# The operands of TensorE's products lie 144 bytes further in SBUF

## The chip, the cores and the metric

The kernel runs on one core of one Trainium2 chip. The time is the device time of one launch in microseconds, from three runs; one more execution is profiled. A core has TensorE (PE in the profile; PEld is its weight load), VectorE (DVE), ScalarE (ACT), GpSimd (POOL) and the queues that issue transfers (SP's above all). SBUF is the on-chip memory of 128 partitions; an address below is a byte offset in each partition.

## The reference, cut to what matters

One inference step over 256 prompt tokens and 32 sample tokens (288 columns in the kernel), through one layer: a feed-forward block, a mixer of two gated recurrences, and a second feed-forward block, each between normalisations, in float32.

```
def swiglu(x, w_in, w_out):
    gate, up = jnp.split(x @ w_in, 2, axis=-1)
    return (jax.nn.silu(gate) * up) @ w_out
...
    x = x + 0.5 * rmsnorm(swiglu(rmsnorm(x, g[0]), ffn1_w_in[l], ffn1_w_out[l]), g[1])
    m, sg, sh = hybrid_mixer(rmsnorm(x, g[2]), mix_w_in[l], ...)
    x = x + rmsnorm(m, g[3])
    x = x + 0.5 * rmsnorm(swiglu(rmsnorm(x, g[4]), ffn2_w_in[l], ffn2_w_out[l]), g[5])
```

The model width is 2048 and the feed-forward width 5632. The change touches none of the arithmetic; it matters only that nearly all work is the matrix products of these three parts.

## The kernel before

**Products in three parts.** A float32 operand is split into a high half (rounded to the type fp32r) and a low half (the rest), and a product is the sum of high by high, high by low and low by high. So every weight tile of 128 x 128 takes part in three matmuls of 128 x 288.

**Units and blocks.** Weights come from HBM in units of 128 x 1024 values (512 KB): two row groups of 128, an even and an odd one, by 512 columns. `Weights.load` (L93) issues the transfer into one of three buffers `raw`; `Weights.pieces` (L120) splits it into one of four buffers `wh`, ScalarE writing the high half (L137) and VectorE the low half (L138). `block` (L626) takes 8 units where the operand is `xhl` (the split input, 16 row groups; the groups gate, up, qk, v, hfq, hi and mo of the profile) and accumulates four PSUM tiles of 128 x 288. For each unit `two` (L640) issues six matmuls per PSUM tile, so 24 per unit, all at L647. The output product of the feed-forward blocks (group out) reads the split hidden tile `hid` instead and takes 2 units per block, over four blocks `o` of output columns; 192 of its matmuls in a row stand for one chunk of 512 hidden columns. An even chunk uses the first two places below, an odd chunk the last two; a few blocks take all four.

**Where the operands lie.** Call 16 bytes (4 values) a line, and count lines within 256 bytes, so 0 to 15. `tiles` (L51) lays out `xhl`, `hid` and the tile for the early products (`fill`) in the same way: the row groups of four successive units start 0, 27, 9 and 18 lines from each other's common start (`PART`, L37), and the reading order of a matmul (`turns_of`, L48) goes through eight places that lie 36 lines apart before it moves on by one line. `Weights.add` (L89) gives the four units of a pass the offsets 7, 2, 0 and 9 lines in their weight buffer (`AHEAD_LINES`, L38). Together with small unused tiles ("gap") at the head of some pools this makes the odd row group's high half begin at the same line in the weights and in the input. For the four units that follow each other these lines are 5, 0, 14 and 7, and then 5 again. The other halves of a unit lie at fixed distances from them, the same for every unit. The weight buffers are 8448 bytes apart, 33 times 256, so that a unit's line does not depend on its buffer.

**What sets the order.** The program is written out by Python once; each engine's instructions stand in that order, and semaphores between engines are placed by the framework from the tiles that are written and read. There is no cost model.

Of the kernel before, what the change touches and what calls it, by code (L numbers as in the profile page):

```python
# [9 lines left out]
F32 = mybir.dt.float32  # L10
F32R = mybir.dt.float32r
# [5 lines left out]
P = 128  # L17
TP = 256
TS = 32
T = TP + TS  # L20
# [13 lines left out]
LINE = 4  # L34
PLACES = 8
# [15 lines left out]
def tiles(pool, n, name):  # L51

    q = n // 2 * T
    t = pool.tile([P, LINE + 10 * LINE + 4 * q], F32R, name=name, tag=name, bufs=1)
    hs, ls = [None] * n, [None] * n
    for dst, odd, at in ((hs, 1, 0), (hs, 0, q + 4 * LINE), (ls, 1, 2 * q + 10 * LINE), (ls, 0, 3 * q + 10 * LINE)):
        r = t[:, LINE + at:LINE + at + q].rearrange("p (b g j c) -> p b g j c", g=PLACES, j=4, c=T // PLACES)
        for u in range(n // 2):
            dst[2 * u + odd] = r[:, u // 4, :, PART[u % 4], :]
    return hs, ls  # L60
# [6 lines left out]
def apart(t, step):  # L67

    return bass.AP(t.tensor, t.offset, [list(t.ap[0]), [step, 2], list(t.ap[1])])


class Weights:
# [47 lines left out]
    def pieces(self, n):  # L120

        i = self.split
        raw = self.raws.pop(i)
        pool = self.extra if i in self.extra_units else self.hlp
        hl = pool.tile([P, 2112], F32R, name=f"wh{i}", tag="wh")
        at = self.at[i]
        low = hl[:, at + ODD_LOW:at + ODD_LOW + 2 * (EVEN_LOW - ODD_LOW)]
        l = low.rearrange("p (a c) -> p a c", a=2)[:, ::-1, 0:512]
        h = apart(hl[:, at:at + 512], ODD_HIGH)
        self.parts[i] = (h, l)  # L130
        self.split += 1
        raw = raw.rearrange("p (a b) -> p a b", b=512)
        for j in range(n):
            a = slice(0, 2) if n == 1 else slice(2 * j // n, 2 * j // n + 1)
            w = min(512, 1024 // n)
            c = slice(j * w % 512, j * w % 512 + w)
            i1 = self.nc.scalar.activation(h[:, a, c], raw[:, a, c], AF.Copy).ins  # L137
            i2 = self.nc.vector.tensor_tensor(l[:, a, c], raw[:, a, c], h[:, a, c].bitcast(F32), op=ALU.subtract).ins  # L138
            self.recent = i1, i2
            yield i1, i2  # L140
# [27 lines left out]
def trunk_kernel(ctx, tc, x_prompt, x_sample, state_gla, state_hgrn, norm_gains, f1_in, f1_out, f2_in, f2_out,  # L168
# [6 lines left out]
    xpool = ctx.enter_context(tc.tile_pool(name="xpool", bufs=1))  # L175
# [69 lines left out]
    def wider(n):  # L245

        return {i for i in range(n - 44, n + 4) if i // 2 % 3 == (n + 2) // 2 % 3}
# [38 lines left out]
    x = [xpool.tile([P, T], F32, name=f"x{k}") for k in range(KT)]  # L286
    yg = [xpool.tile([P, 4, T], F32, name=f"y{k}") for k in range(4)]
    y = [yg[k // 4][:, k % 4, :] for k in range(KT)]
    xh, xl = tiles(xpool, KT, "xhl")
    rt = xpool.tile([P, T], F32, name="rt")  # L290
    rp = xpool.tile([P, T], F32, name="rp")
# [224 lines left out]
    class PreNorm:  # L516
# [3 lines left out]
        def __init__(self, name, update, ahead, at):  # L520

            self.name, self.update, self.ahead, self.at, self.late = name, update, ahead, at, []
            self.tmps = None
# [25 lines left out]
    class Fill:  # L549
# [3 lines left out]
        def __init__(self, pool, name, gains, gnext, some, ahead):  # L553
            self.gnext, self.name, self.some, self.ahead = gnext, name, some, ahead
            pool.tile([P, 8], F32, name=f"{name}gap")

            both = list(zip(*tiles(pool, 2 * EARLY, f"{name}hl")))
            self.tiles = [both[:EARLY], both[EARLY:]]
            self.gains = pool.tile([P, 32], F32, name=f"{name}g")[:, 0:EARLY]
            V.tensor_tensor(self.gains, gains[:, 0:EARLY], prm[:, gnext * KT:gnext * KT + EARLY], op=ALU.mult)  # L560
# [146 lines left out]
    def ffn(tag, gcol, gnext, pn, before, fill=None):  # L707
# [2 lines left out]
        border = []  # L710
        with ExitStack() as pools:
            fp = pools.enter_context(tc.tile_pool(name=f"ffn{tag}", bufs=2))
            fp.tile([P, 32], F32, name=f"gap_f{tag}", bufs=1)
            hid, final_tiles = {}, []
            hidden = tiles(fp, 8, f"hid{tag}")

            def do_in(c):
# [1007 lines left out]
    class Border:  # L1725


        def __init__(self, n, gains, gnext, some, ahead=0):
            self.pools = ExitStack()
            top = self.pools.enter_context(tc.tile_pool(name=f"top{gnext}", bufs=1, side="right"))  # L1730
            top.tile([P, 88], F32, name=f"gap{gnext}")
            W.begin_extra(self.pools.enter_context(tc.tile_pool(name=f"hx{gnext}", bufs=2, side="right")), wider(n))
            self.fill = Fill(self.pools.enter_context(tc.tile_pool(name=f"fl{gnext}", bufs=1, side="right")),
                             f"fill{gnext}", gains, gnext, some, ahead)

    pn = pre1 = PreNorm("pre1", x_first, FIRST, 11)
    pn.late.append(prm2)
    u, border = ffn(1, lambda k: hg1[:, k:k + 1], 2, pn, first)
    u, border = mixer(PreNorm("pre2", u, UPDATED, 11), border)
    ffn(2, lambda k: hg1[:, KT + k:KT + k + 1], None, PreNorm("pre3", u, UPDATED, 11), border.pools, border.fill)  # L1740


# [39 lines left out]
```

## Time and profile before

| what | value |
|---|---|
| median of 3 runs | 2148.63 us (2147.24 to 2149.55) |
| time of the profiled execution | 2147.9 us |
| its span, first to last instruction | 2146.1 us |
| PE busy | 2134.7 us, 99% of the span |
| DVE, ACT busy | 1379.6 us (64%), 1016.8 us (47%) |
| mean granted clock of TensorE | 0.999 |
| matmuls at L647 | 15456 |

The profile's page gives the busy time of each engine, the span in 40 slices, the DMA queues, the chain of work that ended last (followed back from the last instruction), and the costliest groups of instructions. The ends of matmuls are modelled and overlap the next matmul's start, so PE's busy share does not tell how fast it runs; how long a row of matmuls lasts does.

### The profile page before, as it was taken

Reading aid. Unit: us, or ns where it says so; the run is one execution under the profiler, and the core shown is the slowest. Engines: PE = TensorE matmul, PEld = TensorE weight load, DVE = VectorE, ACT = ScalarE, POOL = GpSimd, SP = SyncE. Lnnn points to the kernel's source line nnn. Section 1 sums busy time; section 2 is a strip of 40 time slices with the busy share of each in tenths; the row PEclk is TensorE's granted clock in tenths of the full one; section 3 lists DMA queues with packets and bytes.
Section 4 is the critical chain, followed back from the end, with each engine's and each line's share of the span. In section 5 each row is a group of like instructions: output and inputs, shape, how many; then the busy total and the mean of one; then the engine's idle time right before and its main releaser. Section 6 shows DMA issues by size and latency. Waiting matters only on the chain.

```text
span 2146.1 us, 43224 instructions
## 1 busy us (share of the span) xinstructions
PE 2134.7 (99%) x17828; PEld 2115.5 (99%) x17828; DVE 1379.6 (64%) x2253; ACT 1016.8 (47%) x1537; POOL 180.5 (8%) x327
## 2 busy tenths in 40 slices
PE   9999999999999999999999999999999999999998
PEld 9999999999999999999999999999999999999998
DVE  7655546655665568888888755854665466556656
ACT  6453433343344445655676654644334333433344
POOL 2000000000000001333110000000000020122005
PEclk9999999999999999999999999999999999999999
DMA  7665555555556654678666664555555565666556
GB/s 222 180 177 176 171 176 176 176 171 177 175 176 188 179 175 139 199 211 221 178 188 183 184 190 145 161 176 176 176 177 172 175 186 177 183 186 186 176 171 163
DMA packets 227334, 384.87 MB, mean 179 GB/s; under 512 B 21362, under 2 KB 60864, under 8 KB 227136
## 3 DMA queue, kind: packets, MB, share of 16 engines
q1 hardware_dynamic: 213872, 365.02, 56.7%
q0 software_dynamic: 10992, 16.77, 3.0%
q8 instruction: 140, 2.29, 0.4%
q10 hardware_dynamic: 2272, 0.31, 0.1%
q14 instruction: 58, 0.48, 0.1%
HBM read 363.75 MB, written 11.80 MB: 175 GB/s over the span
## 4 chain that ended last, share of the span: by engine, by line
PE 93%; DVE 3%; ACT 2%; issue 1%; DMA 1%; POOL 0%; DVEq 0%; ACTq 0%; POOLq 0%
PE gate L647 26%; PE out L647 24%; PE up L647 24%; PE hfq L647 5%; PE mo L647 4%; PE hi L647 2%; PE v L647 2%; ACT wh L137 1%; DVE wh L138 1%; PE gate L637 1%; PE gate L636 0%; PE gate L638 0%; PE os L1401 0%; PE sc L1147 0%; ACT ls L202 0%
## 5 line engine op out<-in xcount | busy, mean ns | idle before, releaser
L138 DVE TENSOR_TENSOR wh<-raw,wh 128x1024 fp32r<-128x1024 f32 (+1 forms) x676 | 821.4, 1216 | 572.2 <-ACT wh L137 571.2
L137 ACT ACTIVATE wh<-raw 128x1024 fp32r<-128x1024 f32 (+1 forms) x676 | 709.9, 1052 | 886.5 <-PE gate L647 275.9
L647 PE MATMUL gate<-xhl,wh 128*128 128x288 f32 x4584 | 588.3, 288 | 1.2 <-DVE u L740 0.8
L647 PEld LDWEIGHTS gate<-xhl,wh 128*128 128x128 f32 x4584 | 582.0, 187 | 2.8 <-issue 0.7
L647 PE MATMUL out<-hid,wh 128*128 128x288 f32 x4224 | 532.5, 286 | 0.0
L647 PEld LDWEIGHTS out<-hid,wh 128*128 128x128 f32 x4224 | 530.2, 187 | 0.1
L647 PE MATMUL up<-xhl,wh 128*128 128x288 f32 x4152 | 527.9, 287 | 0.0
L647 PEld LDWEIGHTS up<-xhl,wh 128*128 128x128 f32 x4152 | 525.3, 187 | 0.0
L831 DVE TENSOR_TENSOR y<-out,y 128x288 f32<-128x288 f32 x287 | 116.8, 451 | 73.2 <-PE out L647 73.1
L647 PE MATMUL hfq<-xhl,wh 128*128 128x288 f32 x768 | 103.3, 290 | 0.0
L647 PEld LDWEIGHTS hfq<-xhl,wh 128*128 128x128 f32 x768 | 98.6, 187 | 0.9
L788 POOL DMA_DIRECT2D xT<-b x64 | 37.2, 587 | 733.2 <-PE gate L647 550.6
L647 PE MATMUL mo<-xhl,wh 128*128 128x288 f32 x768 | 97.6, 288 | 0.2 <-ACT y L1715 0.2
L647 PEld LDWEIGHTS mo<-xhl,wh 128*128 128x128 f32 x768 | 97.1, 187 | 0.5 <-ACT y L1715 0.4
L991 POOL MEMSET ahl<- 128x512 f32 x1 | 0.5, 525 | 782.6 <-PE out L647 782.6
L742 ACT ACTIVATE hid<-u 128x288 fp32r<-128x288 f32 x88 | 37.5, 445 | 59.5 <-DVE u L741 58.0
L740 DVE TENSOR_TENSOR u<-up,rt 128x288 f32<-128x288 f32 x88 | 37.8, 451 | 29.2 <-PE up L647 29.2
L647 PE MATMUL hi<-xhl,wh 128*128 128x288 f32 x384 | 53.5, 291 | 0.0
L735 DVE TENSOR_TENSOR g<-gate,rt 128x288 f32<-128x288 f32 x80 | 33.6, 454 | 30.7 <-PE gate L647 30.7
L647 PEld LDWEIGHTS hi<-xhl,wh 128*128 128x128 f32 x384 | 50.2, 188 | 0.5
L647 PE MATMUL v<-xhl,wh 128*128 128x288 f32 x360 | 49.4, 290 | 0.0
L202 ACT ACTIVATE g<-g 128x288 f32<-128x288 f32 x88 | 36.0, 436 | 25.6 <-DVE g L735 25.2
(409 smaller groups left out, 1525.3 us busy)
## 6 DMA issues: line engine op xcount, KB each, us to landing
raw<-in_ffn_w_in_dram SPq DMA_DIRECT2D x350, 512.0 KB, 3.8
raw<-in_ffn_w_out_dram SPq DMA_DIRECT2D x176, 512.0 KB, 3.7
raw<-in_mix_w_in_dram SPq DMA_DIRECT2D x64, 512.0 KB, 4.4
raw<-in_mix_w_in_dram SPq DMA_DIRECT2D x96, 256.0 KB, 3.4
raw<-in_mix_w_out_dram SPq DMA_DIRECT2D x32, 512.0 KB, 3.8
out_dram<-s POOLq DMA_DIRECT2D x32, 256.0 KB, 3.0
s<-in_state_gla_dram SPq DMA_DIRECT2D x16, 256.0 KB, 6.3
s<-in_state_hgrn_dram SPq DMA_DIRECT2D x16, 256.0 KB, 5.8
```

Source lines behind the costliest of these rows:

```text
L137: i1 = self.nc.scalar.activation(h[:, a, c], raw[:, a, c], AF.Copy).ins
L138: i2 = self.nc.vector.tensor_tensor(l[:, a, c], raw[:, a, c], h[:, a, c].bitcast(F32), op=ALU.subtract).ins
L202: ins = S.activation(out, in_, func, **kw).ins
L637: yield lambda: PE.matmul(dst, w[0][:, a, c], parts[1], start=False, stop=False)
L647: product[0] = PE.matmul(dst, w[low][:, a, c], part, start=k == n == 0, stop=k == nk - 2 and n == 5).ins
L735: V.tensor_tensor(g, ps, rt, op=ALU.mult)
L740: ins = V.tensor_tensor(u, ps, rt, op=ALU.mult).ins
L742: S.activation(hh[f], columns(u), AF.Copy)
L788: queues[n % len(queues)].dma_start(dst[q * TS:(q + 1) * TS, 4 * g:4 * g + 4, :, cols].rearrange("p k t c -> p (k t) c"), b32[rows, q])
L831: V.tensor_tensor(y[k], ps, y[k], op=ALU.add)
L991: G.memset(ahl[:, 512:].bitcast(F32), 0.0)
```

## The change

Five lines. The tiles for `xhl`, `hid` and `fill` lose one unused line at their head, and the unused tiles in front of them grow, or one is added (`gap_x`), so that the data begins 144 bytes, which is 9 lines, further than before. Everything in a weight buffer moves one line further inside the buffer, and the buffers themselves move by 128 bytes because of the added tile, so also by 144 bytes. For the tiles at the right end of the memory (`fill` and the extra weight buffers in the pools `hx`) the larger gap moves the address 112 bytes down, which is the same 9 lines within 256 bytes.

| operand | start before | start after | move |
|---|---|---|---|
| `xhl` | 55632 | 55776 | +144 |
| `hid` | 147280 | 147424 | +144 |
| `fill` | 193360 | 193248 | -112 |
| `wh`, first buffer, with its offset of one line after | 108672 | 108816 | +144 |
| extra `wh` in `hx`, first buffer, likewise | 212096 | 211984 | -112 |
| `raw`, first buffer | 96192 | 96320 | +128 |
| `g`, `u` of the feed-forward blocks, `sq`, mixer tiles | | | +128 |
| `x`, `y`, and the mixer's pool `scan` | | | 0 |

The four successive units now begin at lines 14, 9, 7 and 0. Built, the two programs hold the same 24652 instructions in the same order on every engine, with the same shapes, steps and semaphores; only addresses differ (and the numbers in tile names).

```diff
@@ def tiles(pool, n, name):
-    t = pool.tile([P, LINE + 10 * LINE + 4 * q], F32R, name=name, tag=name, bufs=1)
+    t = pool.tile([P, 10 * LINE + 4 * q], F32R, name=name, tag=name, bufs=1)
...
-        r = t[:, LINE + at:LINE + at + q].rearrange("p (b g j c) -> p b g j c", g=PLACES, j=4, c=T // PLACES)
+        r = t[:, at:at + q].rearrange("p (b g j c) -> p b g j c", g=PLACES, j=4, c=T // PLACES)
@@ Weights.pieces
-        at = self.at[i]
+        at = LINE + self.at[i]
@@ trunk_kernel
+    xpool.tile([P, 40], F32, name="gap_x")
     xh, xl = tiles(xpool, KT, "xhl")
@@ ffn
-            fp.tile([P, 32], F32, name=f"gap_f{tag}", bufs=1)
+            fp.tile([P, 40], F32, name=f"gap_f{tag}", bufs=1)
@@ Border
-            top.tile([P, 88], F32, name=f"gap{gnext}")
+            top.tile([P, 120], F32, name=f"gap{gnext}")
```

## The prediction

> **What bounds the kernel now.** I read the page first, its busy times and the chain that ended last.
>
> ```profile
> span 2146.1 us, 43224 instructions
> PE 2134.7 (99%) x17828; PEld 2115.5 (99%) x17828; DVE 1379.6 (64%) x2253; ACT 1016.8 (47%) x1537; POOL 180.5 (8%) x327
> PE 93%; DVE 3%; ACT 2%; issue 1%; DMA 1%; POOL 0%; DVEq 0%; ACTq 0%; POOLq 0%
> ```
>
> TensorE is the bound nearly throughout, and it hardly waits: the span less its busy time is 11.4 us. So the time can move only if a matmul takes longer or shorter. The groups of instructions tell how many there are: all L647 groups that read `xhl`, and the one that reads `hid`.
>
> ```profile
> L647 PE MATMUL gate<-xhl,wh 128*128 128x288 f32 x4584 | 588.3, 288 | 1.2 <-DVE u L740 0.8 <-ACT xhl L300 0.5
> L647 PE MATMUL out<-hid,wh 128*128 128x288 f32 x4224 | 532.5, 286 | 0.0
> L647 PE MATMUL up<-xhl,wh 128*128 128x288 f32 x4152 | 527.9, 287 | 0.0
> L647 PE MATMUL hfq<-xhl,wh 128*128 128x288 f32 x768 | 103.3, 290 | 0.0
> L647 PE MATMUL mo<-xhl,wh 128*128 128x288 f32 x768 | 97.6, 288 | 0.2 <-ACT y L1715 0.2
> L647 PE MATMUL hi<-xhl,wh 128*128 128x288 f32 x384 | 53.5, 291 | 0.0
> L647 PE MATMUL v<-xhl,wh 128*128 128x288 f32 x360 | 49.4, 290 | 0.0
> L647 PE MATMUL qk<-xhl,wh 128*128 128x288 f32 x216 | 29.1, 290 | 0.0
> ```
>
> Those that read `xhl` add up to 4584 + 4152 + 768 + 768 + 384 + 360 + 216 = 11232. Four units of 24 matmuls are a pass, so that is 117 passes; an up or gate block is two. The chain in order of time shows that blocks with equal work differ in length:
>
> ```profile
> 375.42 24.21 PE up L647 x192
> 399.63 23.98 PE out L647 x192
> 423.61 24.23 PE gate L647 x192
> 447.84 24.21 PE up L647 x192
> 472.05 24.03 PE out L647 x192
> ```
>
> Each row is 192 matmuls of one form. An up block takes 24.21 us, an out group of an even chunk 23.98, one of an odd chunk 24.03. To see why, I cut the up block at 375 us at the first matmul of each unit of its first pass, whose lines are 5, 0, 14 and 7 (columns: the stretch, its length, PE's busy time and the count of matmuls that touch it, the granted clock, DMA).
>
> ```profile
> 375.25:378.25 3.00, 3.00 (x24) 1.00 0.59 175
> 378.25:381.24 2.99, 2.99 (x27) 1.00 0.59 175
> 381.24:384.32 3.08, 3.08 (x26) 1.00 0.58 176
> 384.32:387.36 3.04, 3.04 (x26) 1.00 0.54 172
> ```
>
> The same 24 matmuls take 3.00 us at line 5, 2.99 at 0, 3.08 at 14 and 3.04 at 7, 12.11 together, and the second pass brings the block to the 24.21 of the chain. The clock is 1.00 in all four and the DMA share alike, so it is not the clock. The counts run over 24 because a matmul's modelled end reaches into the next unit; the cuts are at starts. The out groups show the same lines in other company: the even chunk goes 5, 0, 5, 0 and the odd one 14, 7, 14, 7.
>
> ```profile
> 399.47:402.46 2.99, 2.99 (x24) 1.00 0.56 181
> 402.46:405.45 2.99, 2.99 (x26) 1.00 0.12 28
> 405.45:408.47 3.02, 3.02 (x27) 1.00 0.79 246
> 471.89:474.88 2.99, 2.99 (x24) 1.00 0.56 182
> 474.88:477.90 3.02, 3.02 (x27) 1.00 0.12 30
> ```
>
> Here the unit at 14 follows one at 7 and takes 2.99, not 3.08. So the slow unit is no property of line 14 alone, but of 14 **after** 0: I read it as a state that TensorE's reads carry from one unit into the next.
>
> **The change part by part.** No instruction is added, removed or moved, so no count times duration changes by itself.
>
> Moving `raw` by 128 bytes and the results of gate and up by 128, with `x` and `y` left in place, alters what ScalarE and VectorE read beside what they write. Their share of a unit is covered:
>
> ```profile
> L138 DVE TENSOR_TENSOR wh<-raw,wh 128x1024 fp32r<-128x1024 f32 (+1 forms) x676 | 821.4, 1216 | 572.2 <-ACT wh L137 571.2
> L137 ACT ACTIVATE wh<-raw 128x1024 fp32r<-128x1024 f32 (+1 forms) x676 | 709.9, 1052 | 886.5 <-PE gate L647 275.9 <-PE up L647 230.2 <-PE out L647 225.2
> ```
>
> ACT's 1.05 us and then DVE's 1.22 make 2.27 us of a unit's 2.99, four buffers deep; both would have to slow by a third together before TensorE waited. I take 0. Without the cover, a tenth on either row would be 71 or 82 us in all, but I have no row that lets an address cost that.
>
> What is left is TensorE's own reading, the weights and the input moved alike by 9 lines. How each differs from its neighbour stays: the distances between successive units are again -5, -2, -7 and -2 lines. What changes is whether a unit begins on an even or an odd line, because 9 is odd. I sort the rows above by that:
>
> - odd to even, 5 to 0 and 7 to 14: the later unit takes 2.99 both times, in passes and out groups, though the distances differ;
> - even to odd, 14 to 7 and 0 to 5 in the out groups: 3.02 both times; after the slow unit, 3.04;
> - odd to odd, 7 to 5, two lines back: 3.00;
> - even to even, 0 to 14, two lines back: 3.08.
>
> The new pass goes 14, 9, 7, 0. From 14 to 9 is even to odd, 9 to 7 odd to odd and two lines back, 7 to 0 odd to even, 0 to 14 even to even and the very pair of lines that is slow now. One jump of each kind stands before and after. So 14, first in the pass, takes 3.08; 9 follows a slow unit and takes 3.04; 7 takes 3.00 and 0 takes 2.99. The sum is 12.11 a pass, a difference of 0.00 over 117 passes. The out groups go 14, 9, 14, 9 and 7, 0, 7, 0: one even to odd (3.02) and one odd to even (2.99) in each pair, 6.01 as in the rows now; again 0.00. What the trace does not show is 14 to 9 and 7 to 0, whose distances (-5 and -7) are swapped among the kinds. Bounds for either: 2.99 (nothing lost) to 3.08 (the slowest unit seen), so -0.05 to +0.04 for line 9 against 3.04, and 0 to +0.09 for line 0 against 2.99. I take 3.04 and 2.99, the nearest rows of their kind. Over 117 passes the ends are -5.9 and +15.2 us.
>
> The sum: the profiled execution's own 2147.9 us, of which 1.8 lie around the span, plus 0 for the passes, the out groups and the covered engines. The median of the runs stands 0.7 above the profiled time, so I forecast **2148.6 us**.
>
> The Trainium skill speaks against any effect. "SBUF — State Buffer", section "Who interferes with whom", gives PE two read ports of its own and says that PE and ACT never wait on anyone; its Specifications count in lines of 16 bytes, of which 144 is a multiple. By these the units could not differ and the change would do nothing. The trace disagrees on the first point, with 2.99 against 3.08 us for the same work, so for this kernel the rows decide; the time by the rule would be the same 2148.6.
>
> **The rivals.**
>
> *The slow unit goes away (faster).* Its place: the start of a pass. For it: 14 after 7 takes 2.99 and 7 after that takes 3.02, and the jump from 0 to 14 now stands where a pass begins, its predecessor reached by another way (7, then 0). Against it: the pair of lines is the same, and by its end the unit at 0 should be in the same state. If 14 costs 2.99 and 9 costs 3.02, a pass saves 0.09 + 0.02 = 0.11, over 117 passes 12.9 us: 2135.7.
>
> *A second unit is slow (slower).* Its place: the unit at line 0 after 7, or that at 9 after a slow 14. Two even lines are needed for the 3.08 in the rows, and the unit at 7 behind it is nearly back at 3.02. If 0 falls into it after 7, which no row shows, it costs 3.08 in place of 2.99, 0.09 a pass, 10.5 us: 2159.1; were the out groups of the odd chunks (8 of the 22 that 4224 matmuls make, four such units each) slow too, 2.9 more, 2162.0. It decides as soon as that unit is nearer 3.08 than 2.99. Against it: both odd-to-even rows are at 2.99.
>
> *The address does not matter by itself.* The units would differ by something that moves with them, their distances alone, and every row comes back as it is: 2148.6.
>
> **How the numbers follow.** The forecast (one jump of each kind, the slow unit first in the pass) gets 0.41, the address without effect 0.12, the slow unit gone or mostly gone 0.27, a second slow unit or a longer row of slow matmuls 0.20. 0.2% is 4.3 us, about what a measurement of this kernel can tell from no change, and twice the spread of its three runs (2.3 us). The forecast's own range, with small differences in 14 to 9 and 7 to 0, is 2144 to 2153; it leaves that 4.3 us seldom, and I move 0.08 of it to the two sides, evenly. So faster is 0.31, same 0.45, slower 0.24. The range that holds the time 8 times in 10 must reach towards both prices: 2135 to 2160, short of the worst of the slower case and of a gain beyond the first rival's.
>
> **What would show it.** Right: in an up block at 24.2 us the first unit takes 3.08, the second 3.04, the third 3.00, the fourth 2.99; out groups at 23.98 to 24.05 in the chain. The first rival: up blocks near 24.0, no unit above 3.02. The second: up blocks above 24.3, with two units near 3.08, or out groups above 24.2. Address without effect: up blocks 24.21 with the third unit slow, as now. The whole argument falls if L137 or L138 change their means by over a tenth, if TensorE's idle time grows beyond 11.4 us, or if a new kind of unit appears above 3.08.

## The result, and the profile after

The median is 2137.35 us over four runs (2136.51 to 2140.21), against 2149.09 over four runs of the kernel before (2147.24 to 2149.63). The ratio is 0.9949 with a 95% interval of 0.9933 to 0.9965: the change makes the kernel faster by 0.5%, or 11.7 us. The profiled execution took 2136.5 us. In the changed kernel's numbering everything behind the added tile stands one line lower in the file, so L647 has become L648.

The page of the changed kernel: span, busy times, and the groups that read `xhl` or `hid`. The two figures behind the bar are busy microseconds and the mean of one in ns.

```profile
span 2134.7 us, 43224 instructions
PE 2123.4 (99%) x17828; PEld 2103.9 (99%) x17828; DVE 1378.7 (65%) x2253; ACT 1015.9 (48%) x1537; POOL 180.0 (8%) x327
L138 DVE TENSOR_TENSOR wh<-raw,wh 128x1024 fp32r<-128x1024 f32 (+1 forms) x676 | 821.4, 1216 | 565.9 <-ACT wh L137 564.7
L137 ACT ACTIVATE wh<-raw 128x1024 fp32r<-128x1024 f32 (+1 forms) x676 | 709.3, 1051 | 878.5 <-PE gate L648 271.8
L648 PE MATMUL gate<-xhl,wh 128*128 128x288 f32 x4584 | 583.1, 286 | 0.8 <-DVE u L741 0.8
L648 PE MATMUL out<-hid,wh 128*128 128x288 f32 x4224 | 532.7, 286 | 0.4 <-DVE y L832 0.4
L648 PE MATMUL up<-xhl,wh 128*128 128x288 f32 x4152 | 522.9, 286 | 0.0
L648 PE MATMUL hfq<-xhl,wh 128*128 128x288 f32 x768 | 103.2, 290 | 0.0
L648 PE MATMUL mo<-xhl,wh 128*128 128x288 f32 x768 | 96.8, 287 | 0.3 <-ACT y L1716 0.2
L648 PE MATMUL hi<-xhl,wh 128*128 128x288 f32 x384 | 53.3, 291 | 0.0
L648 PE MATMUL v<-xhl,wh 128*128 128x288 f32 x360 | 49.5, 290 | 0.0
```

The span fell by 11.4 us and PE's busy time by 11.3, so the gain is all in the matmuls. The splitting of the weights (L137, L138) is as before to the nanosecond or one beside it, and PE's idle time is 11.3 us as it was 11.4. The gain has two rows: gate fell from 588.3 to 583.1 and up from 527.9 to 522.9; mo gave 0.8 more. The mixer's groups hfq and hi gained 0.1 and 0.2, v lost 0.1, and out lost 0.2. The chain in order of time shows the same by blocks of 192 matmuls (start, length, what).

```profile
372.72 23.97 PE up L648 x192
396.69 23.94 PE out L648 x192
420.63 23.98 PE gate L648 x192
...
468.57 24.19 PE out L648 x192
```

Up and gate blocks are at 23.97 and 23.98 where they were at 24.21 to 24.23. The out group of an even chunk went from 23.98 to 23.94, that of an odd chunk from 24.03 to 24.19. The up block, cut at the first matmul of each unit of its first pass (lines 14, 9, 7 and 0), and two units of an out group of an odd chunk (lines 0 and 7):

```profile
372.55:375.55 3.00, 3.00 (x25) 1.00 0.56 175
375.55:378.54 2.99, 2.99 (x27) 1.00 0.60 175
378.54:381.53 2.99, 2.99 (x26) 1.00 0.57 181
381.53:384.54 3.01, 3.01 (x26) 1.00 0.55 174
...
471.45:474.46 3.01, 3.01 (x27) 1.00 0.14 22
474.46:477.50 3.04, 3.04 (x26) 1.00 0.80 261
```

No unit of a pass is slow any more: 11.99 us for the four, where it was 12.11. The clock is 1.00 in all of them, as before. The 3.04 of the unit at line 7 after line 0 is the loss in the odd chunks; before, the unit at that place took 2.99.

### The profile page after: what moved, and what is told of

Its sections match the earlier page's. It is cut to its first block, busy times and chain, and to the rows that moved or that the text cites. A ratio compares the mean times of both kernels' runs of the same rounds, so it can differ in the third digit from the quotient of the medians.

```text
span 2134.7 us, 43224 instructions
## 1 busy us (share of the span) xinstructions
PE 2123.4 (99%) x17828; PEld 2103.9 (99%) x17828; DVE 1378.7 (65%) x2253; ACT 1015.9 (48%) x1537; POOL 180.0 (8%) x327
## 4 chain that ended last, share of the span: by engine, by line
PE 93%; DVE 3%; ACT 2%; DMA 1%; issue 1%; ACTq 0%; DVEq 0%; SPq 0%
PE gate L648 26%; PE out L648 24%; PE up L648 23%; PE hfq L648 5%; PE mo L648 3%; PE hi L648 2%; PE v L648 2%; ACT wh L137 1%; DVE wh L138 1%; PE gate L638 1%; PE gate L637 1%; PE gate L639 1%; DMA raw<-in_mix_w_out_dram 0%; DMA raw<-in_ffn_w_out_dram 0%; PE os L1402 0%
## 5 line engine op out<-in xcount | busy, mean ns | idle before, releaser
L138 DVE TENSOR_TENSOR wh<-raw,wh 128x1024 fp32r<-128x1024 f32 (+1 forms) x676 | 821.4, 1216 | 565.9 <-ACT wh L137 564.7
L137 ACT ACTIVATE wh<-raw 128x1024 fp32r<-128x1024 f32 (+1 forms) x676 | 709.3, 1051 | 878.5 <-PE gate L648 271.8
L648 PE MATMUL gate<-xhl,wh 128*128 128x288 f32 x4584 | 583.1, 286 | 0.8 <-DVE u L741 0.8
L648 PEld LDWEIGHTS gate<-xhl,wh 128*128 128x128 f32 x4584 | 576.9, 187 | 2.1 <-issue 0.7
L648 PE MATMUL out<-hid,wh 128*128 128x288 f32 x4224 | 532.7, 286 | 0.4 <-DVE y L832 0.4
L648 PEld LDWEIGHTS out<-hid,wh 128*128 128x128 f32 x4224 | 530.3, 187 | 0.6 <-DVE y L832 0.6
L648 PE MATMUL up<-xhl,wh 128*128 128x288 f32 x4152 | 522.9, 286 | 0.0
L648 PEld LDWEIGHTS up<-xhl,wh 128*128 128x128 f32 x4152 | 520.2, 187 | 0.0
L648 PE MATMUL hfq<-xhl,wh 128*128 128x288 f32 x768 | 103.2, 290 | 0.0
L648 PEld LDWEIGHTS hfq<-xhl,wh 128*128 128x128 f32 x768 | 98.5, 187 | 1.0
L648 PE MATMUL mo<-xhl,wh 128*128 128x288 f32 x768 | 96.8, 287 | 0.3 <-ACT y L1716 0.2
L648 PEld LDWEIGHTS mo<-xhl,wh 128*128 128x128 f32 x768 | 96.3, 187 | 0.7 <-ACT y L1716 0.7
L648 PE MATMUL hi<-xhl,wh 128*128 128x288 f32 x384 | 53.3, 291 | 0.0
L648 PEld LDWEIGHTS hi<-xhl,wh 128*128 128x128 f32 x384 | 50.1, 188 | 0.6
L648 PE MATMUL v<-xhl,wh 128*128 128x288 f32 x360 | 49.5, 290 | 0.0
```

The source lines that it names most:

```text
L648: product[0] = PE.matmul(dst, w[low][:, a, c], part, start=k == n == 0, stop=k == nk - 2 and n == 5).ins
```

## The experiments

All of them are built from the kernel before unless said otherwise, and all ratios are to that kernel, with 95% intervals. Unit times in the text below are from the start of a unit's first matmul to that of the next unit; the median is taken over all passes of a run. The theories are these. **A**: what decides is whether the lines are odd or even. **B**: the exact places decide, above all 0 followed by 14. **C**: it is not TensorE's operands but the 128 bytes by which `raw` and the results of gate and up moved. **D**: weights and input stand in a relation within 512 bytes. **E**, formed on what A's runs showed: a slow unit is a state that TensorE carries over from the matmuls just ahead.

### One line, and no tile moved

```diff
 def tiles(pool, n, name):
-    t = pool.tile([P, LINE + 10 * LINE + 4 * q], F32R, name=name, tag=name, bufs=1)
+    t = pool.tile([P, 2 * LINE + 10 * LINE + 4 * q], F32R, name=name, tag=name, bufs=1)
-        r = t[:, LINE + at:LINE + at + q].rearrange("p (b g j c) -> p b g j c", g=PLACES, j=4, c=T // PLACES)
+        r = t[:, 2 * LINE + at:2 * LINE + at + q].rearrange("p (b g j c) -> p b g j c", g=PLACES, j=4, c=T // PLACES)
 Weights.pieces
-        at = self.at[i]
+        at = LINE + self.at[i]
```

> Only what TensorE reads moves, by one line (16 bytes) inside its tiles; no tile moves, so raw, g, u, x and y stay where they were. The units start at lines 6, 1, 15 and 8. Theory A (odd against even: the slow unit is the third one after a second one on an even line, so a move by any odd number of lines removes it): the pass falls from 12.11 to about 11.99 us, an up block is near 23.97 us, no unit above 3.02 in the passes, the kernel near 2137. Theory B (the places themselves: the second unit at line 0, the third beyond the end of the 256 bytes, at 14): the step from 1 to 15 still goes over the end of the 256 bytes, so up blocks stay near 24.2 us and the kernel near 2149. Theory C (it was the 128 bytes by which raw and the results of gate and up moved): nothing of these moves here, so 24.21 and 2149.

Measured: 2137.04 us, ratio 0.9951 (0.9936 to 0.9965). Its chain:

```profile
372.68 23.97 PE up L647 x192
396.65 23.94 PE out L647 x192
...
468.53 24.19 PE out L647 x192
```

Each of these blocks has the length that it has in the changed kernel, the slower out group of odd chunks among them, though the lines are 6, 1, 15 and 8 and not 14, 9, 7 and 0. Theory C falls, since nothing but TensorE's operands moved by these 16 bytes. Theory B falls too: the step over the end of the 256 bytes is still taken from the second to the third unit, and that unit takes 3.00.

### Eight lines

```diff
+    xpool.tile([P, 32], F32, name="gap_x")
     xh, xl = tiles(xpool, KT, "xhl")
...
-            top.tile([P, 88], F32, name=f"gap{gnext}")
+            top.tile([P, 120], F32, name=f"gap{gnext}")
```

> Everything from the split input on moves 128 bytes, that is 8 lines, by a gap alone; raw, g and u move as in the change, and the units start at lines 13, 8, 6 and 15: every line keeps its parity. Theory A (odd against even): the third unit is slow again, up blocks 24.21 us, the kernel near 2149. Theory B (the places): no unit is at line 0 followed by 14, so the third takes 3.00, up blocks near 24.0, the kernel 2136 to 2140. Theory C (the move of raw, g and u by 128 bytes): up blocks 23.97, near 2137.

Measured: 2148.5 us, ratio 1.0001 (0.9992 to 1.0011). The units start at lines 13, 8, 6 and 15; this is the third of a pass of an up block:

```profile
381.21:384.29 3.08, 3.08 (x26) 1.00 0.61 176
```

The third unit, at line 6, takes the 3.08 that line 14 took. Almost everything that the change moved by 144 bytes moved by 128 here, and the whole gain is gone: the last 16 bytes carry it.

### Two lines

The moves so far were by 1, 9 and 8 lines. Odd and even explain them, but so would a pattern that comes back every 4 or 8 lines.

```diff
+    xpool.tile([P, 8], F32, name="gap_x")
     xh, xl = tiles(xpool, KT, "xhl")
...
-            top.tile([P, 88], F32, name=f"gap{gnext}")
+            top.tile([P, 144], F32, name=f"gap{gnext}")
```

> Everything from the split input on moves 32 bytes, two lines (units at 7, 2, 0 and 9). The moves tried so far were by 1, 9 and 8 lines, which odd against even explains, but so would a pattern that repeats every 4 or 8 lines. Theory A (odd against even, nothing else of the line): every unit as before, the third at 3.08, up blocks 24.21, out groups 23.98 and 24.03, 2149. Rival (a period of 4 or 8 lines): some unit differs from both patterns seen, up blocks anywhere from 23.95 to 24.3 and not 24.21, or out groups off 23.98 and 24.03.

Measured: 2148.06 us, ratio 0.9999 (0.9989 to 1.0008).

```profile
375.98 24.21 PE up L648 x192
400.20 23.98 PE out L648 x192
...
472.62 24.03 PE out L648 x192
```

These rows, and the gate and up blocks left out (24.23 and 24.21), are those of before. So of the four moves of all operands together, 1 and 9 lines give one kernel, and 2 and 8 lines give the other, which is that of before. Theory A holds for them; no other move was tried.

### Weights against the input, 256 bytes

```diff
-    hlp.tile([P, 48], F32, name="gap_w", bufs=1)
+    hlp.tile([P, 112], F32, name="gap_w", bufs=1)
```

> The weight buffers, the hidden tile and the results of gate and up move by 256 bytes, the split input and raw do not: all lines within 256 bytes are those of before. Theories A and B, which know only lines within 256 bytes: 24.21 us for an up block and 2149, as before. Theory D (what counts is where a weight lies against the input within 512 bytes): up and gate blocks change, by up to 0.25 us either way (2137 if the slow unit goes, 2160 if another becomes slow), while out groups, whose two operands move alike, stay at 23.98 and 24.03.

Measured: 2148.08 us, ratio 1.0000 (0.9990 to 1.0009). Up and gate blocks are at 24.21 to 24.23 and the out groups at 23.98 and 24.03, as before. Theory D falls.

### The first run again, with `raw` shifted

`raw` gets four more columns, of which the first four stay unused, and `gap_w` shrinks by what the three buffers take more, so that the weights stay where the first run has them. The hunks of the first run are not repeated.

```diff
-        raw = self.rawp.tile([P, 1024], F32, name=f"raw{i}", tag="raw")
+        raw = self.rawp.tile([P, 1028], F32, name=f"raw{i}", tag="raw")[:, 4:]
...
-    hlp.tile([P, 48], F32, name="gap_w", bufs=1)
+    hlp.tile([P, 24], F32, name="gap_w", bufs=1)
```

> The first of these runs once more, with TensorE's operands at the same places, but the raw data 16, 48 and 80 bytes further in its three buffers. Theories A and B: the same as that run in every unit, within 0.02 us a unit. Theory C (the relation of what TensorE reads to what ScalarE and VectorE read of raw): the passes differ from that run's by up to 0.12 us each, 14 us in all.

Measured: 2149.93 us, ratio 1.0011 (1.0001 to 1.0020): 13 us above the run it repeats, which neither side had. But the units are as in that run to 0.01 us, and so are the blocks of its chain (up 23.97, out 23.94 and 24.19). What was lost lies in the mixer, and the waits of SP's queue show why (line that waits, waited for, us in total, times, longest):

```profile
SPq L97 <- DMA raw<-in_mix_w_in_dram: 114.7, 48, 3.7
```

In the first run that row reads 0.5 us in one time. L97 issues a unit of the mixer in two halves; with the tile shifted the second half waits for the first, as many times as there are such units, so that they reach L137 and L138 later. I take the loss for this side effect of the experiment; it was not tried apart. The profiled execution, at 2144.64 us, was the fastest of its ten, so the trace holds only about half of the 13 us. For the passes themselves theory C falls a second time.

### Weights alone, input alone

```diff
 weights alone, in Weights.pieces
-        at = self.at[i]
+        at = LINE + self.at[i]
 input alone, in tiles
-    t = pool.tile([P, LINE + 10 * LINE + 4 * q], F32R, name=name, tag=name, bufs=1)
+    t = pool.tile([P, 2 * LINE + 10 * LINE + 4 * q], F32R, name=name, tag=name, bufs=1)
-        r = t[:, LINE + at:LINE + at + q].rearrange("p (b g j c) -> p b g j c", g=PLACES, j=4, c=T // PLACES)
+        r = t[:, 2 * LINE + at:2 * LINE + at + q].rearrange("p (b g j c) -> p b g j c", g=PLACES, j=4, c=T // PLACES)
```

> Only the weights move, by one line inside their buffers; the split input and the hidden tile stay. If the weights' line carries the odd-or-even effect: up blocks 23.97 us, 2137. If the input's line carries it: up blocks 24.21, 2149. If it is the two together (both on one line, odd or even): neither, and units that were at 2.99 become slower, since weights and input no longer begin on the same line: up blocks above 24.3 and the kernel above 2155.

> The counterpart: the split input, the hidden tile and the tile of the early products move by one line, the weights stay. Weights' line: up blocks 24.21, 2149. Input's line: 23.97, 2137. The two together: slower than before, up blocks above 24.3, kernel above 2155.

Measured: 2204.71 us, ratio 1.0267 (1.0247 to 1.0288), for the weights alone, and 2200.38, ratio 1.0247 (1.0226 to 1.0267), for the input alone. One row of each, in that order:

```profile
385.67 24.98 PE up L647 x192
```

```profile
384.50 24.88 PE up L647 x192
```

All units of the up, gate and out blocks are slow now, at medians of 3.08 to 3.14 us. So it takes both operands, and a line between them costs 57 and 52 us, over four times what the change moved. Which of the two carries odd and even can't be told this way, since taking them apart brings a larger loss of its own. The Trainium skill, "SBUF — State Buffer", section "Who interferes with whom", calls PE's two read ports, one for the moving operand and one for the weights, independent. If that settled the time of a matmul, 16 bytes between its two operands would cost nothing. The traces disagree: an up block takes 24.98 or 24.88 us in place of 24.21.

### The same round of lines, handed out one unit later

```diff
-PART = (0, 3, 1, 2)
-AHEAD_LINES = (7, 2, 0, 9)
+PART = (2, 0, 3, 1)
+AHEAD_LINES = (9, 7, 2, 0)
```

> Places as before, but handed out one unit later: a pass now starts at lines 7, 5, 0, 14 in place of 5, 0, 14, 7; the round is the same, only which unit of a block has which line differs. If a unit's line and its way there (5, 0, then 14) decide, the fourth unit of a pass takes 3.08, the first 3.04, the sum stays 12.11, up blocks 24.2, kernel 2146 to 2152. If the number of the unit in the pass decides (its row group, its weight buffer), the third unit, now at line 0, takes 3.08. The out groups of odd chunks now go 0, 14, 0, 14, so that 14 follows a 0 that was reached by going up two lines: 3.08 there (groups of 192 near 24.4) if the pair 0 to 14 is enough, 3.02 or less (24.0) if 0 has to be reached from 5.

Measured: 2152.61 us, ratio 1.0019 (1.0009 to 1.0029). The four units of a pass (lines 7, 5, 0, 14), and a unit at line 14 of an out group of an odd chunk (0, 14, 0, 14):

```profile
375.56:378.59 3.03, 3.03 (x24) 1.00 0.55 173
378.59:381.59 3.00, 3.00 (x26) 1.00 0.60 175
381.59:384.58 2.99, 2.99 (x27) 1.00 0.62 175
384.58:387.66 3.08, 3.08 (x26) 1.00 0.57 173
...
475.70:478.69 2.99, 2.99 (x26) 1.00 0.16 39
```

The slow unit went along to the fourth place: it is not the number of the unit that decides. And the pair is not enough: in the out group 14 after 0 takes 2.99, where that 0 was reached by going up from 14; in the pass the 0 was reached from 5, and 14 takes 3.08. It is not the kind of group either. An out group that takes all four places, so with `hid` alone as input, starts at lines 0, 14, 7 and 5 and has both cases. These are two of its units at 14, both after 0: the first, whose 0 stands behind the 14 that ended the up block, and the second, whose 0 stands behind a 5.

```profile
767.01:770.01 3.00, 3.00 (x27) 1.00 0.17 37
...
779.01:782.09 3.08, 3.08 (x26) 1.00 0.53 178
```

The passes keep their sum. The total lies just above the 2146 to 2152 that I had expected, and the reason was not among the theories. The loss of 4.6 us is in the even chunks' out groups, which now go 7, 5, 7, 5 and take 24.53 in place of 23.98, nine times (9 x 0.55 = 5.0). The row of one, and its units at the third, the fifth and the seventh place, all three at line 7 after line 5:

```profile
399.93 24.53 PE out L647 x192
...
405.80:408.92 3.12, 3.12 (x26) 1.00 0.75 249
...
412.04:415.06 3.02, 3.02 (x26) 1.00 0.60 178
...
418.06:421.18 3.12, 3.12 (x27) 1.00 0.58 168
```

The step from 5 to 7, two lines up between odd lines, occurs in no pass and no out group of the kernel before or after. But it does not cost the same each time. The eight units go 3.04, 2.99, 3.12, 3.12, 3.02, 3.00, 3.12 and 3.12: in the second and the fourth pair the unit at 5 is as slow as the one at 7, in the third neither is. The lines ahead of the fifth and of the seventh unit are the same (7, 5, 7, 5), so a few lines back do not tell the cost either. What else differs between the pairs was not tried apart.

### Two matmuls change places

```diff
             six = [(0, 1, oh), (0, 1, ol), (0, 0, eh), (1, 1, oh), (0, 0, el), (1, 0, eh)]
+            if nk == KT and k % 8 == 2 and f == nf - 1:
+                six[4], six[5] = six[5], six[4]
```

> All addresses as before. In each second unit of a pass the last two of its 24 matmuls change places, so that the third unit, at line 14, follows a matmul on other halves of the tiles; the products are the same. If the slow unit is a state that TensorE carries over from the matmuls just before (theory E), the third unit leaves 3.08: 2.99 to 3.04, the pass loses 0.04 to 0.11, the kernel 2136 to 2145. If its own line and its predecessor's line decide whatever comes between, it stays at 3.08 and the kernel at 2149, or above by what the swap costs itself.

Measured: 2143.58 us, ratio 0.9980 (0.9970 to 0.9989). The third and the fourth unit of a pass, and then the third alone, in its four stretches of six matmuls. The second fence shows the same four stretches in the kernel before.

```profile
380.48:383.49 3.01, 3.01 (x26) 1.00 0.61 174
383.49:386.54 3.05, 3.05 (x27) 1.00 0.52 177
...
380.48:381.25 0.77, 0.77 (x8) 1.00 0.28 35
381.25:382.00 0.75, 0.75 (x9) 1.00 0.73 112
382.00:382.74 0.74, 0.74 (x8) 1.00 1.04 399
382.74:383.49 0.75, 0.75 (x8) 1.00 0.42 158
```

```profile
381.24:382.00 0.76, 0.76 (x9) 1.00 0.20 35
382.00:382.78 0.78, 0.78 (x8) 1.00 0.72 158
382.78:383.54 0.76, 0.76 (x9) 1.00 1.01 377
383.54:384.32 0.78, 0.78 (x8) 1.00 0.41 134
```

Here all addresses are those of before, and the third unit runs its own 24 matmuls in the same order. All that differs is the order of the last two matmuls ahead of it, and it takes 3.01 in place of 3.08. The stretches show what kind of difference it is. Before, the unit goes 0.76, 0.78, 0.76, 0.78 to its end; after the swap it loses a little in the first stretch and then runs at 0.75. So the same reads can settle into two rhythms, and what ran just before decides which. That is theory E for the third unit. The fourth stays at 3.05, so its 3.04 of before did not come from the slow unit ahead of it.

### The swap on the changed kernel, and in two units

The first of these is the changed kernel with the swap of the run above; the second is the kernel before with `k % 8 in (2, 4)`.

> The changed kernel with the same swap as in the run before the last: the last two matmuls of each second unit of a pass change places. If the swap itself sets how the next unit starts (theory E), the third unit costs what it cost with the swap on the old lines, 3.01, and the second 3.00 in place of 2.99, so odd or even lines no longer matter there: up blocks 24.01, the kernel 2139 to 2141. If the swap only helped by undoing something of the even line, the third unit stays at 3.00 and up blocks at 23.97 to 23.99. If the state can be entered from an odd line too, the third unit goes to 3.08 and up blocks to 24.2.

> The kernel before, addresses as there, with the swap of the last two matmuls in the second and in the third unit of a pass. Theory E: as the swap took the third unit from 3.08 to 3.01, the one in the third unit takes the fourth, at line 7, from 3.04 to 3.02 or less: up blocks 24.05 or less (24.09 with one swap), the kernel 2139 to 2142. If the fourth unit's 3.04 goes by its line alone: 24.09 or more, the kernel 2143 to 2145.

Measured: 2138.98 us, ratio 0.9954 (0.9939 to 0.9969), for the changed kernel with the swap, where up blocks stay at 23.97. The second and the third unit of a pass:

```profile
376.62:379.62 3.00, 3.00 (x27) 1.00 0.59 175
379.62:382.61 2.99, 2.99 (x27) 1.00 0.62 181
```

The second unit pays 0.01 for the swap and the third gains 0.01. The number that I had put on theory E here, 3.01, did not come: with the swap the third unit still starts better from the odd line (2.99) than from the even one (3.01). So the swap does not replace the address; on the old lines it only keeps the unit out of the slow rhythm.

The kernel before with two swaps took 2143.16 us, ratio 0.9975 (0.9965 to 0.9984); its third and fourth unit:

```profile
379.85:382.88 3.03, 3.03 (x27) 1.00 0.65 178
382.88:385.89 3.01, 3.01 (x26) 1.00 0.53 174
```

The fourth unit fell from 3.05 to 3.01 (3.02 as the median over the passes), as theory E has it. But the swap cost the third unit 0.02 itself, so the up block only came to 24.08 and not to 24.05, and the kernel missed the 2139 to 2142 of theory E: half of that expectation failed.

### The out groups back on the old lines

The odd chunks' out groups lose 0.16 us each in the changed kernel. This run keeps the split input and its weights one line further, as in the first run, and puts `hid` and the weights of the out groups back on the lines of before.

```diff
-def tiles(pool, n, name):
+def tiles(pool, n, name, lead=2 * LINE):
...
-            hidden = tiles(fp, 8, f"hid{tag}")
+            hidden = tiles(fp, 8, f"hid{tag}", LINE)
...
-        self.at.append(LINE * AHEAD_LINES[k // 2 % 4])
+        self.at.append(LINE * (more + AHEAD_LINES[k // 2 % 4]))
...
-                    block_units(w_out, o * 512, 4 * c, 4 * n)
+                    block_units(w_out, o * 512, 4 * c, 4 * n, more=0)
```

> The split input and its weights one line further (lines 6, 1, 15, 8), but the hidden tile and the weights of the out groups on their lines of before (5, 0 and 14, 7). If each unit's cost goes by its own line and the one or two units ahead (theory A), both halves come out separately: up and gate blocks 23.97 us, out groups of even chunks 23.98 and of odd chunks 24.03. Against the change that is 9 times 0.04 more and 8 times 0.16 less, 0.9 us: 2136.4, the best of all, by less than can be measured in the total. Rival: where the lines change parity between a block and an out group, the first units go wrong; then up blocks or out groups are over these values, 24.1 or more.

Measured: 2137.61 us, ratio 0.9949 (0.9934 to 0.9964).

```profile
396.76 23.97 PE out L647 x192
420.73 24.01 PE gate L647 x192
...
468.71 24.06 PE out L647 x192
492.77 23.99 PE gate L647 x192
```

Both halves come out separately: up blocks at 23.97 (among the rows left out) and out groups near their old values. But the gate block behind an out group pays 0.03 and 0.02 for the passage (24.01 for 23.98, 23.99 for 23.97), and the odd chunks' groups come back to 24.06 and not to 24.03. And the two out groups that take all four places, which the expectation left out, have their slow units back: 48.44 and 46.90 us where the changed kernel has 48.02 and 46.52. By these blocks nothing is left of the 0.9 us, and no version beats the change by more than the measurement can tell.

## Why the prediction was right and wrong

**What bounds the kernel.** Right. PE's busy time fell by 11.3 us and the span by 11.4, with the granted clock at 0.999 before and after.

**The cover of ScalarE and VectorE.** Right: 1051 and 1216 ns, against 1052 and 1216 before, and PE's idle time did not grow.

**The start lines decide, and TensorE carries a state from one unit into the next.** Right, and now shown: all operands moved together by 1 or 9 lines make one kernel, by 2 or 8 lines the other, and a swap of two matmuls takes the third unit out of the slow rhythm with no address changed.

**"One jump of each kind stands before and after."** This is the step that failed. I sorted the jumps by the lines that they go between, odd or even, and took it that a jump of the same kind costs the same again; the pair 0 to 14 above all, "the very pair of lines that is slow now". Predicted and measured for a pass:

| unit at | predicted | measured (median) |
|---|---|---|
| 14, after 0 | 3.08 | 2.99 |
| 9, after 14 | 3.04 | 2.99 |
| 7, after 9 | 3.00 | 3.00 |
| 0, after 7 | 2.99 | 3.01 |
| sum | 12.11 | 11.99 |

The pair of lines alone does not tell the cost; the way to the first line belongs to it. The slow jump before was two lines back between even lines, from a unit that had been reached by five lines back. After the change the jump two lines back between even lines (0 to 14) comes behind one of seven lines back, and the one that comes behind five lines back (9 to 7) is between odd lines. Neither is slow. That the out groups' unit at 14 took 2.99 after 7 was read as a sign of a carried state, and then this state was left out of the sorting, but for the unit right behind a slow one. The run that hands the round out one unit later shows how far that goes: even the same four lines ahead (7, 5, 7, 5) were followed by 3.02 and by 3.12.

**The out groups.** Predicted as unchanged; the even chunks' gained 0.04 and the odd chunks' lost 0.16. The text had "one even to odd (3.02) and one odd to even (2.99)". Even to odd came out on both sides of that, 2.99 from 14 to 9 and 3.04 from 0 to 7; odd to even was off by 0.01 to 0.02, with 3.00 from 9 to 14 and 3.00 to 3.01 from 7 to 0. The range that I gave for the two jumps not shown (2.99 to 3.08) holds them, but I had left the out groups out of it.

**The first rival, the slow unit gone.** This is what happened, and nearly at its price: 2135.7 against 2137.35. The measured time lies within 2135 to 2160 only because that range reached towards this price; the forecast's own 2144 to 2153 does not hold it. Its reason was the one that the runs bear out, a predecessor reached by another way. Two things in its sum were off and partly cancelled. A pass saved 0.12 and not 0.11; but it does not save it 117 times. The groups hfq, hi, v and qk make 18 of the 117 passes (1728 of 11232 matmuls), and these four gained 0.3 us together. That leaves 99 passes, 11.9 us; the out groups take 8 x 0.16 and give 9 x 0.04, which is 0.9 net. So 11.0, against 11.3 of PE's busy time. Three out groups are in neither count: the two that take all four places go like passes and fell from 48.41 to 48.02 and from 46.87 to 46.52, and one of an even chunk rose from 24.19 to 24.64. Nothing should be read into the last, which takes 23.98 to 25.62 us in the runs with the even chunks' lines of before. Why the mixer's passes gain so little was not tried. The traces show that they hardly occur as such: other products stand between their matmuls, and of those 1728 only one row is as long as a pass, 139 matmuls of hfq. It fell from 17.61 to 17.46 us, about what 139 matmuls of unbroken passes gain.

**The second rival, a second slow unit.** It did not come in the passes; the unit at 0 after 7 takes 3.01. A part of it came in the out groups of odd chunks, where the unit at 7 after 0 takes 3.04 and not 3.08.

**Address without effect.** Refuted by the first run, in which 16 bytes inside the tiles give 0.9951. By the rule of the Trainium skill cited in the prediction ("SBUF — State Buffer", "Who interferes with whom") the units could not differ at all, and all these runs would have come out at the time of before; for two operands 16 bytes apart the rule misses 2.5 to 2.7%.

**What stays open.** No run shows what in the chip holds the state, nor why it tells odd lines of 16 bytes from even ones. The costs of the other jumps are measured and not explained; two lines up from 5 to 7 takes 3.02 or 3.12 with the same lines ahead of it.

## What to carry to other kernels

When TensorE is busy throughout, cut its time at the starts of equal pieces of work: pieces that differ at the same clock point to where the operands lie, and a move of both operands by 16 bytes is a cheap trial. Try it at an odd and at an even number of lines, and keep weights and input on the same line, since one line between them cost 52 to 57 us here and the change gained 11.7. Don't carry the cost of one step over to another by its two ends alone; what ran before it belongs to it, further back than one unit, so a sum over such steps is a guess until it has been run.

## What the runs showed that was not expected

- The effect of moving both operands together fits a period of 32 bytes as far as it was tried: 2 and 8 lines give ratios of 0.9999 and 1.0001, 1 and 9 lines 0.9951 and 0.9949.
- Weights and input one line apart cost 2.5 to 2.7% of the kernel, in every unit of the up, gate and out blocks.
- The same 24 matmuls at the same addresses take 3.08 or 3.01 us, by the order of two matmuls ahead of them.
- Units that go back and forth between lines 7 and 5 alternate by pairs between 3.00 and 3.12 us, and 3.12 is more than the slow unit of before.
